# Eight tokens per one-hot operation, a 32-token top-k tile stacked on four partition sets, and early expert splits on GpSimd

## The chip, the cores and the metric

The kernel runs on one core of one Trainium2 chip. The core has five engines with queues of their own: TensorE (PE, with its weight load PEld), VectorE (DVE), ScalarE (ACT), GpSimd (POOL) and SyncE (SP, which here only issues DMAs). Each engine works through its queue in order and waits on semaphores for the others. The metric is the device time of one execution, in microseconds (us).

## What is computed

One layer of a decoder is run for 1024 prompt positions and 8 x 4 sample positions, 1056 tokens of 1024 features in all. A mixing part (RWKV-7 and a pooling part) comes first, then a PEER layer of 16384 single-neuron experts, then a gate and a last norm. The change lies in the PEER layer:

```python
q  = (xb @ wq).reshape(n, 8, 2, 128)             # 8 heads, two halves
s1 = einsum('thc,nc->thn', q[:, :, 0], sub_keys[0]); s2 = ... q[:, :, 1], sub_keys[1]
v1, i1 = top_k(s1, 16); v2, i2 = top_k(s2, 16)   # 16 of 128 keys, twice
cand = v1[..., :, None] + v2[..., None, :]       # 256 sums
sc, ci = top_k(cand.reshape(n, 8, 256), 16)      # 16 of them
expert = i1[ci // 16] * 128 + i2[ci % 16]
gate = softmax(sc)
act = gelu(einsum('thkd,td->thk', u_tab[expert], xb)) * gate
out = einsum('thk,thkd->td', act, v_tab[expert])
```

## The kernel before

The tokens stand in four groups (0-288, 288-544, 544-800, 800-1056; the sample comes first). For the first 672 tokens (`GA` to `GB`) the expert layer is done densely: a matrix G of 16384 experts x 672 tokens holds the gates, all experts are multiplied with all these tokens on PE, and G masks the result. For the other 384 tokens the chosen rows of the tables are gathered from memory by GpSimd and multiplied on DVE.

Ahead of the dense part three streams of work run interleaved (`merge`, lines 926 to 934, takes the next piece of the stream that is least far along by its stated length): `b_stream`, the RWKV chunks; `phase_c` of one group (output projection, norm, query projection, key scores, which go to memory in `sc_d`); and `t_stream` of the group before. `t_stream` runs `top` and `select` for each tile of up to 128 tokens that is dense: tiles of 128, 128 and 32 tokens in group 0, two of 128 in group 1, and one of 128 in group 2 (group 2 has 128 dense tokens). What was written in this order is then ordered anew by a scheduler when the program is built, engine by engine.

`top` (line 753) has the tokens on the partitions. For each of 16 rows of scores (8 heads x 2 halves) DVE takes eight largest, finds their places, strikes them out, takes the next eight and finds those: five operations (lines 762 to 767). `select` (line 772) builds 50 candidates a head (`cand` on DVE, their codes on GpSimd), finds 16 of them (lines 802 to 808, six operations a head), puts them in order of the code (lines 813 to 816, three a head), makes the softmax, and brings each gate to its place with a small one-hot `oh` (line 847 on DVE, then a product on GpSimd, then a sum at line 850).

For a dense tile the two key numbers and the gate of the 128 choices of each token are transposed on PE (line 863), so that the choices are on the partitions, and rounded to 16 bits (`e16`, the gate as a high and a low part). Then G is built four tokens at a time (lines 873 to 890): DVE compares a row 0..127 with both key numbers (line 882, 1024 elements a partition), multiplies the one-hot of the second key by the high part of the gate (line 883, 512 elements), and a third operation multiplies it by the low part (line 884, 512 elements). `GLO(t)` (line 1051) gives that one to DVE for every third set of four tokens and to GpSimd (the helper `PTT`, whose operations all have line 124) for the others. PE multiplies the one-hots, two matmuls a token (line 887), ACT moves the result out of PSUM into `gst` (line 889), and 32 tokens at a time it goes to `g_d` in memory (line 891). `ab`, the tile of the one-hots, has three buffers.

The dense part (`dense`, line 1170) takes 128 blocks of 128 experts. A block's `ublock` splits the weights into a high and a low part (`esplit`, line 1065: ACT makes `ehi`, and `elo` is made on DVE, line 1071, or on GpSimd), multiplies with all 672 tokens (`emm`, line 1093) and applies the GELU (line 1099). `ugate` multiplies by the rows of G (line 1150, loaded from `g_d` as `gq`) and splits again (`wh` on ACT, `wl` on DVE, line 1154). After eight blocks come eight `vblock`s. The first eight `ublock`s (`upre`) are run before G is complete, with GpSimd making `elo`; their results lie in `OT0` to `OT7`, of which `OT7` is in the pool `late`, in memory that the one-hot tiles give up. `gtop` runs `top` for the gathered tokens, three tiles of 128: the first before `dense(0, 18)` in the program, the two others after it.

## Time and profile before

| | us |
|---|---|
| median of 3 runs | 3357.13 |
| their range | 3352.67 to 3357.15 |
| the profiled execution | 3346.63 |
| its span, first to last instruction | 3344.9 |
| TensorE's granted clock, mean of the span | 0.98 |

The profile is of one execution. Its page gives the busy time of each engine and, in 40 equal slices of the span, the busy share in tenths. Times of day below are counted from the span's start. A matmul's record reaches to its end, and matmuls overlap, so a busy PE need not be one at its peak. A record of a DVE or GpSimd operation also holds the time in which it was started and could not go on.

In words: the mixing part and the first group's projections take the first 715 us; from there to 1394 us the streams run with `top`, `select` and the one-hots among them; from 1394 to 3230 us the dense part runs; a tail of norms and gates ends at 3345 us.

### The profile page before, as it was taken

The page shows a single profiled execution, that of the slowest core. Times are in us where ns is not written, and L with a number is a line of the kernel's source. Part 1 is how long each engine was busy: PE and PEld are TensorE (multiplying, and loading weights), DVE is VectorE, ACT ScalarE, POOL GpSimd, SP SyncE. Part 2 cuts the span into 40 slices and gives each one's busy share as a digit, 9 for nine tenths or more (in the row PEclk, how much of TensorE's full clock was granted, in tenths as well). Part 3 has the DMA queues.
Part 4 walks back from the last instruction along what each step waited for, and adds up shares of the span by engine and source line. Part 5 has one row for each costly group of instructions (what it writes and reads, how often), then busy time and mean ns, then how long its engine had stood idle before and what let it go on. Part 6 is the DMA issues. An engine that isn't in the chain of part 4 may idle for free.

```text
span 3344.9 us, 57622 instructions
## 1 busy us (share of the span) xinstructions
PE 3163.4 (95%) x21831; PEld 3063.6 (92%) x21831; DVE 2661.9 (80%) x5365; ACT 1187.9 (36%) x1778; POOL 1803.7 (54%) x1434
## 2 busy tenths in 40 slices
PE   8997999998888888999999999999999999999997
PEld 7886989988878777899999999999999999999997
DVE  6777332359999989889888888888889888888966
ACT  6452523345555555431222222122122222222243
POOL 5434333235565456337666666666566666666635
PEclk9998999999999989999999999999999999999998
DMA  5568645667677787639999999999999999999933
GB/s 176 204 218 199 170 134 144 196 193 228 199 198 232 207 290 222 233 128 366 341 339 328 344 349 331 329 340 334 336 337 350 325 335 339 342 328 341 324 110 128
DMA packets 467861, 883.61 MB, mean 264 GB/s; under 512 B 129280, under 2 KB 252416, under 8 KB 463104
## 3 DMA queue, kind: packets, MB, share of 16 engines
q1 hardware_dynamic: 356992, 477.24, 44.3%
q0 software_dynamic: 110592, 402.70, 32.8%
q8 instruction: 171, 2.80, 0.3%
q14 instruction: 106, 0.87, 0.1%
HBM read 759.22 MB, written 120.60 MB: 263 GB/s over the span
## 4 chain that ended last, share of the span: by engine, by line
PE 69%; DVE 16%; DMA 4%; POOL 2%; issue 2%; ACT 1%; SPq 0%; DVEq 0%; ACTq 0%; POOLq 0%
PE pd L1093 57%; DVE ab L882 3%; DVE ab L883 2%; PE ps L663 1%; PE ps L661 1%; PE ps L662 1%; PE ps L526 1%; DMA sraw<-wq 1%; PE ps L521 1%; DVE oh L847 1%; DVE h L718 1%; DVE I L763 1%; DVE s L765 1%; DVE ab L884 1%; DVE I L767 1%
## 5 line engine op out<-in xcount | busy, mean ns | idle before, releaser
L1202 POOL DMA_INDIRECT row<-v,idx x384 | 543.4, 1415 | 314.2 <-DVE po L1219 142.6
L1202 POOL DMA_INDIRECT row<-u,idx x384 | 536.4, 1397 | 284.9 <-DVE row L1210 112.3
L1069 ACT ACTIVATE ehi<-eraw 128x1024 fp32r<-128x1024 f32 x278 | 295.0, 1061 | 1098.3 <-PE pd L1093 955.2
L1093 PE MATMUL pd<-XH,elo 128*128 128x336 f32 x2176 | 516.2, 318 | 6.1 <-DVE elo L1071 3.2
L1093 PE MATMUL pd<-XL,ehi 128*128 128x336 f32 x2176 | 515.4, 318 | 0.0
L1093 PE MATMUL pd<-XH,ehi 128*128 128x336 f32 x2176 | 512.5, 316 | 0.0
L1093 PE MATMUL pd<-wh,ehi 128*128 128x336 f32 (+1 forms) x2112 | 503.0, 317 | 6.2 <-DVE tg L1283 6.2
L1093 PE MATMUL pd<-wl,ehi 128*128 128x336 f32 (+1 forms) x2112 | 503.1, 317 | 0.0
L1093 PE MATMUL pd<-wh,elo 128*128 128x336 f32 (+1 forms) x2112 | 503.0, 317 | 0.0
L1219 DVE SCALAR_TENSOR_TENSOR po<-row,act,po 128x1024 f32<-128x1024 f32 x381 | 488.5, 1282 | 6.5
L1210 DVE SCALAR_TENSOR_TENSOR row<-row,xt 128x1024 f32<-128x1024 f32 x384 | 455.2, 1220 | 5.9 <-DMA row<-u,idx 5.8
L1071 DVE TENSOR_TENSOR elo<-eraw,ehi 128x1024 fp32r<-128x1024 f32 x256 | 318.3, 1243 | 79.8 <-ACT ehi L1069 67.8
L1093 PEld LDWEIGHTS pd<-XH,elo 128*128 128x128 f32 x2176 | 373.8, 189 | 7.8 <-DVE elo L1071 4.3
L1093 PEld LDWEIGHTS pd<-XH,ehi 128*128 128x128 f32 x2176 | 373.0, 189 | 0.3
L1093 PEld LDWEIGHTS pd<-XL,ehi 128*128 128x128 f32 x2176 | 371.2, 189 | 0.2
L1093 PEld LDWEIGHTS pd<-wh,ehi 128*128 128x128 f32 x2112 | 361.5, 188 | 6.9 <-issue 6.7
L1093 PEld LDWEIGHTS pd<-wh,elo 128*128 128x128 f32 x2112 | 362.0, 188 | 0.2
L1093 PEld LDWEIGHTS pd<-wl,ehi 128*128 128x128 f32 x2112 | 361.8, 188 | 0.0
L124 POOL TENSOR_TENSOR ab<-ab,e 128x512 f16<-128x512 f16 x110 | 132.0, 1202 | 160.8 <-DVE ab L883 127.5
L1162 DVE TENSOR_TENSOR OT<-pd,OT 128x672 f32<-128x672 f32 x120 | 102.9, 857 | 139.6 <-PE pd L1093 138.0
L889 ACT ACTIVATE gst<-ps 128x512 f32<-128x512 f32 x168 | 177.1, 1093 | 74.0 <-PE ps L887 72.8
L661 PE MATMUL ps<-hi,whi 128*128 128x256 f32 (+1 forms) x592 | 180.0, 305 | 12.0 <-DMA whi<-wc_d 7.4
(504 smaller groups left out, 5849.7 us busy)
## 6 DMA issues: line engine op xcount, KB each, us to landing
eraw<-uT SPq DMA_DIRECT2D x128, 512.0 KB
eraw<-vP SPq DMA_DIRECT2D x128, 512.0 KB
g_d<-gst SPq DMA_DIRECT2D x21, 2048.0 KB
gq<-g_d SPq DMA_DIRECT2D x32, 1344.0 KB
whi<-wc_d SPq DMA_DIRECT2D x148, 256.0 KB
wlo<-wc_d SPq DMA_DIRECT2D x148, 256.0 KB
wc_d<-shi SPq DMA_DIRECT2D x40, 256.0 KB
wc_d<-slo SPq DMA_DIRECT2D x40, 256.0 KB
```

The lines of the kernel that those rows point to most:

```text
L124: nc.gpsimd.tensor_tensor(out, a, b, op=op)
L661: mm(ps[:, :n], whi[:, kk, :], xhi[:, k, :n], start=k == 0, stop=False)
L882: TT(ab[:, 0:4], iota16[:, None, :, :].to_broadcast([128, 4, EB, 2]), pairs(0, 4), op=ALU.is_equal)
L883: TT(ab[:, 4:6], ab[:, 2:4], pairs(2, 2), op=ALU.mult)
L889: ACT(st[:, :, t2:t2 + 4].rearrange("p e t -> p t e"), v3(ps, 128), AF.Copy, scale=1.0 / GS)
L1069: ACT(hi, raw, AF.Copy)
L1071: sub(lo, raw, hi.bitcast(F32), op=ALU.subtract)
L1093: mm(ps[:, a, :n], w_[:, k, :], x_[:, s:s + n], start=first, stop=last)
L1162: TT(halves(OT[db]), ps[:, :, :NH], halves(OT[db]), op=ALU.add)
L1202: nc.gpsimd.indirect_dma_start(out=r[:m], out_offset=None, in_=io[tab], in_offset=bass.IndirectOffsetOnAxis(ap=idx[:m, hh, k:k + 1], axis=0))
L1210: STT(r[:m], r[:m], 1.0, xt[:m], op0=ALU.mult, op1=ALU.mult, accum_out=pre[:m, k:k + 1])
L1219: STT(po[:m], r[:m], act[:m, k:k + 1], po[:m], op0=ALU.mult, op1=ALU.add)
```

## The change

Three things are changed, and one place in memory with them.

The one-hots are built for eight tokens an operation (`GT8`): the comparison has 2048 elements a partition, each product 1024. The third operation always goes to GpSimd, and `GLO` is gone. `ab` is twice as large and has two buffers in place of three. PE has as many matmuls as before and ACT as many moves, two PSUM banks for each set of eight.

The 32-token tile is stacked (`SH` = 4): the scores of two heads at a time lie on a set of 32 partitions, four sets on 128, so that `top` and `select` run over two heads in place of eight, on 128 partitions. Before the transposition the four sets are spread out into a zeroed tile `blk` (eight small ACT moves, one GpSimd memset), and three matmuls with `setsum`, a sum of four pieces of the identity, take the place of the three transpositions. Tiles of 128 tokens are done as before.

`dense(0, 18)` makes `elo` and `wl` on GpSimd (`PTT`) where DVE made them; the later blocks are as before. `OT6` joins `OT7` in `late`, since the larger `ab` leaves less memory. The length that `merge` is told for a tile falls from 24 + m/4 to 24 + m/8.

```diff
-    def top(tk, pos, m):
+    def top(tk, pos, mt):
+        src = sc_d[TIDX[pos]]
+        if mt > TC:
+            m, nh, loads = mt, HEADS, [(slice(0, mt), 0)]
+        else:
+            m, nh = mt * SH, HEADS // SH
+            loads = [(slice(g * mt, (g + 1) * mt), 2 * nh * g) for g in range(SH)]
-        for i in range(16):
+        for i in range(2 * nh):
...
-        for hh in range(HEADS):
+        for hh in range(nh):
...
+        if mt < m:
+            blk = tk.tile([128, HEADS, NCAND], F32, name="blk", tag="code").rearrange("p a b -> p (a b)")[:, :384]
+            nc.gpsimd.memset(blk, 0.0)
+            for g in range(SH):
+                r, c = slice(g * mt, (g + 1) * mt), slice(g * npr, (g + 1) * npr)
+                ACT(blk[r, 0:2, c], e12[r, :, :npr], AF.Copy)
+                ACT(v3(blk[r, 2, c], TOPK), gl[r, :nh, :], AF.Copy)
...
+                mm(ps[:, i * 128:i * 128 + mt], blk[:, i, :], setsum, start=True, stop=True)
...
-            for t2 in range(0, TC, 4):
+            for t2 in range(0, TC, GT8):
-                ab = gp.tile([128, 6, EB, 2], F16, name="ab", bufs=3)
+                ab = gp.tile([128, 3 * nb, EB, 2], F16, name="ab", bufs=2)
-                TT(ab[:, 0:4], iota16[:, None, :, :].to_broadcast([128, 4, EB, 2]), pairs(0, 4), op=ALU.is_equal)
-                TT(ab[:, 4:6], ab[:, 2:4], pairs(2, 2), op=ALU.mult)
-                GLO(t)(ab[:, 2:4], ab[:, 2:4], pairs(3, 2), op=ALU.mult)
+                TT(ab[:, 0:2 * nb], iota16[:, None, :, :].to_broadcast([128, 2 * nb, EB, 2]), pairs(0, 2), op=ALU.is_equal)
+                TT(ab[:, 2 * nb:], ab[:, nb:2 * nb], pairs(2, 1), op=ALU.mult)
+                PTT(ab[:, nb:2 * nb], ab[:, nb:2 * nb], pairs(3, 1), op=ALU.mult)
...
-    def GLO(t):
-        return PTT if t % 12 else TT
...
-            OT[db] = (dr if db < KB - 1 else late).tile([128, ND], F32, name=f"OT{db}")
+            OT[db] = (dr if db < KB - 2 else late).tile([128, ND], F32, name=f"OT{db}")
...
-        TT(wl, wt_, wh.bitcast(F32), op=ALU.subtract)
+        sub(wl, wt_, wh.bitcast(F32), op=ALU.subtract)
-    def vblock(g, db):
-        w = esplit(io["vP"][g, db])
+    def vblock(g, db, sub=TT):
+        w = esplit(io["vP"][g, db], sub)
...
-    dense(0, NB0)
+    dense(0, NB0, PTT)
```

The scheduler orders the program anew. The line numbers of the changed kernel are 2 to 25 higher for the same code. Up to the first tile of `t_stream` the engines have the same order but for the three small DVE operations that make `setsum`. Three places follow, of the kernel before first and then of the changed one.

GpSimd, about 1170 us in the profile before, where the one-hots of the last tile of group 1 run with little else (`ab` is the third one-hot product, `lo` and `sa` belong to `phase_c`, `elo` to the first expert blocks):

```order
L124 TENSOR_TENSOR X<-X,s__12346 128x256
L124 TENSOR_TENSOR yo<-yo,vgb 128x256
L124 TENSOR_TENSOR ab<-ab,e_12632 128x512 x12
L124 TENSOR_TENSOR lo<-y,hi 128x256 x3
L124 TENSOR_TENSOR ab<-ab,e_12632 128x512
L124 TENSOR_TENSOR lo<-y,hi 128x256
L124 TENSOR_TENSOR ab<-ab,e_12632 128x512
L124 TENSOR_TENSOR elo<-eraw,ehi 128x1024 x2
```
```order
L126 TENSOR_TENSOR X<-X,s__11905 128x256
L126 TENSOR_TENSOR ab<-ab,e_12323 128x1024
L126 TENSOR_TENSOR yo<-yo,vgb 128x256
L126 TENSOR_TENSOR ab<-ab,e_12323 128x1024 x9
L126 TENSOR_TENSOR lo<-y,hi 128x256 x2
L126 TENSOR_TENSOR ab<-ab,e_12323 128x1024
L126 TENSOR_TENSOR lo<-y,hi 128x256 x2
L126 TENSOR_TENSOR elo<-eraw,ehi 128x1024 x2
```

The products are twice as long. Eleven of them, for 88 tokens, stand where fourteen stood; those were for some 85 tokens, since every third set of four was DVE's.

ACT behind the last move of one-hots out of PSUM (`gst`), about 1362 us in the profile before (`q` and `scs` belong to `phase_c` of the last group, `ehi` to the weight splits, `OT` to the GELU of the first eight blocks):

```order
L889 ACTIVATE gst_13792<-ps_13891 128x4x128
L1069 ACTIVATE ehi_15047<-eraw_15045 128x1024
L742 ACTIVATE q_14806<-ps_14970 128x256
L750 ACTIVATE scs_15001<-ps_14996 128x512
L750 ACTIVATE scs_15009<-ps_15004 128x512
L1069 ACTIVATE ehi_15080<-eraw_15078 128x1024
L742 ACTIVATE q_15012<-ps_15019 128x256
L1069 ACTIVATE ehi_15136<-eraw_15134 128x1024
L742 ACTIVATE q_15012<-ps_15051 128x256
L1069 ACTIVATE ehi_15168<-eraw_15166 128x1024
L1099 ACT_TABLE_LOAD
L1099 ACTIVATE OT7_15132<-pd_15077 128x672
```
```order
L913 ACTIVATE gst_13321<-ps_13408 128x4x128
L1094 ACTIVATE ehi_14528<-eraw_14526 128x1024
L744 ACTIVATE q_14319<-ps_14394 128x256
L744 ACTIVATE q_14319<-ps_14362 128x256
L1094 ACTIVATE ehi_14560<-eraw_14558 128x1024
L744 ACTIVATE q_14319<-ps_14483 128x256
L1124 ACT_TABLE_LOAD
L1124 ACTIVATE OT6_14475<-pd_14420 128x672
L752 ACTIVATE scs_14514<-ps_14509 128x512
L752 ACTIVATE scs_14522<-ps_14517 128x512
L1094 ACTIVATE ehi_14593<-eraw_14591 128x1024
L744 ACTIVATE q_14525<-ps_14532 128x256
```

`OT6` now comes behind the last one-hots as well, and in all seven moves of `q` are left behind them where five were.

GpSimd in the early dense part, where the gathers of the first tile of gathered tokens begin (`oh` belongs to `gtop`, `row` is a gathered row of a table, `elo` and `wl` are the splits of the expert blocks):

```order
L124 TENSOR_TENSOR code<-code,iotaC 128x400
L124 TENSOR_TENSOR oh<-oh,gt 128x256 x8
L1202 DMA row<-u,idx_15448 128x1024 x16
L1202 DMA row<-v,idx_15448 128x1024 x16
L1202 DMA row<-u,idx_15448 128x1024 x16
```
```order
L126 TENSOR_TENSOR oh<-oh,gt 128x256
L1227 DMA row<-u,idx_14961 128x1024 x7
L126 TENSOR_TENSOR elo<-eraw,ehi 128x1024
L126 TENSOR_TENSOR wl<-wt,wh 128x672
L1227 DMA row<-u,idx_14961 128x1024 x2
L126 TENSOR_TENSOR elo<-eraw,ehi 128x1024
L1227 DMA row<-u,idx_14961 128x1024
L126 TENSOR_TENSOR wl<-wt,wh 128x672
L1227 DMA row<-u,idx_14961 128x1024 x4
L126 TENSOR_TENSOR elo<-eraw,ehi 128x1024
L126 TENSOR_TENSOR wl<-wt,wh 128x672
L1227 DMA row<-u,idx_14961 128x1024 x2
```

Where gathers followed gathers, fourteen `elo` and seven `wl` now stand among the first 53 of them; nine gathers and one `wl` later the gathers run alone as before.

## Rows read from the trace of the kernel before

**Rows 1.** The page: DVE's busy tenths in 40 slices of the span
```profile
DVE  6777332359999989889888888888889888888966
```

**Rows 2.** Busy us (x instructions) by stretch: PE, PEld, DVE, ACT, POOL; clock, DMA
```profile
715.00:1394.00 679.00, 582.93 (x5032) 543.39 (x5033) 628.19 (x2470) 368.24 (x587) 367.24 (x355) 0.96 0.75 227
1394.00:1510.00 116.00, 113.94 (x742) 113.41 (x740) 105.97 (x492) 42.33 (x58) 33.82 (x43) 1.00 0.38 136
1510.00:3230.00 1720.00, 1720.00 (x11205) 1719.95 (x11206) 1484.23 (x1769) 428.35 (x517) 1088.57 (x772) 1.00 0.91 331
```

**Rows 3.** The chain that ended last, 715 to 1394 us: shares by engine and line
```profile
by line: DVE ab L882 15.4%; DVE ab L883 9.0%; issue 4.4%; DVE oh L847 3.7%; DVE I L763 3.0%; DVE s L765 2.7%; DVE ab L884 2.7%; DVE I L767 2.7%; PE ps L887 2.5%; PE pd L1093 2.3%; DVE h L718 2.3%; DVE V L762 2.2%; DVE V L766 2.0%; DVE gl L8
```

**Rows 4.** What PE waited for, 715 to 1394 us: us in all, times, longest
```profile
PE ps L887 <- DVE ab L883: 28.5, 28, 3.0
PE ps L887 <- DVE ab L884: 10.8, 17, 1.3
PE ps L887 <- POOL ab L124: 9.9, 19, 2.4
```

**Rows 5.** Groups by line, 715 to 1394 us: busy us, mean ns, idle before
```profile
L882 DVE TENSOR_TENSOR ab<-iota,e 128x1024 f16<-128x1024 f16 x168 | 145.7, 878 | 15.7 <-PE ps L887 13.4 <-POOL ab L124 2.0
L883 DVE TENSOR_TENSOR ab<-ab,e 128x512 f16<-128x512 f16 x168 | 92.5, 561 | 0.3
L884 DVE TENSOR_TENSOR ab<-ab,e 128x512 f16<-128x512 f16 x58 | 35.0, 604 | 0.2
...
L124 POOL TENSOR_TENSOR ab<-ab,e 128x512 f16<-128x512 f16 x110 | 132.0, 1202 | 160.8 <-DVE ab L883 127.5 <-DVE K L816 10.1 <-DVE SC L806 6.5
```

**Rows 6.** By source line, whole span: ns shortest/median/longest, first and last start
```profile
L882 DVE TENSOR_TENSOR ab<-iota,e x168: 660/686/2337, 765.9 to 1353.7; 128x1024 f16<-128x1024 f16 x168
L883 DVE TENSOR_TENSOR ab<-ab,e x168: 390/416/2293, 772.8 to 1356.5; 128x512 f16<-128x512 f16 x168
...
L124 POOL TENSOR_TENSOR ab<-ab,e x110: 1030/1064/3525, 776.5 to 1357.1; 128x512 f16<-128x512 f16 x110
L124 POOL TENSOR_TENSOR elo<-eraw,ehi x22: 2349/2410/3056, 1200.5 to 3320.0; 128x1024 fp32r<-128x1024 f32 x22
```

**Rows 7.** Timeline, POOL and DVE at 1345 us: start us, us, instruction
```profile
1345.35 1.04 POOL L124 TENSOR_TENSOR ab<-ab,e 128x512 f16<-128x512 f16 x1 [1.02 <-DVE ab L883]
...
1345.46 1.48 DVE L882 TENSOR_TENSOR ab<-iota,e 128x1024 f16<-128x1024 f16 x1
```

**Rows 8.** The chain's pieces in order of time, 1340 to 1400 us: start, us
```profile
1347.60 0.33 DVE oh L847
1347.94 0.33 DVE ab L883
...
1350.69 0.87 DVE V L762 x4
...
1353.20 1.20 DVE ab L882 x2
...
1355.46 0.79 DVE I L763 x3
...
1363.69 8.04 DMA g_d<-gst
1372.16 10.03 DMA gq<-g_d
```

**Rows 9.** DVE's groups of the 32-token tile, 860 to 960 us: busy us, mean ns
```profile
L847 DVE TENSOR_TENSOR oh<-cF,CF 32x256 f32<-32x256 f32 x8 | 5.3, 677 | 0.2
L767 DVE FIND_INDEX8 I<-V,s 32x8 uint32<-32x128 f32 x16 | 4.3, 272 | 0.0
...
L850 DVE TENSOR_REDUCE gl<-oh 32x16 f32<-32x256 f32 x8 | 3.2, 399 | 0.0
...
L807 DVE FIND_INDEX8 CI<-SC,s 32x8 uint32<-32x50 f32 x8 | 1.5, 192 | 0.0
```

**Rows 10.** The page: one of the two groups of gathers: busy us, mean ns, idle before
```profile
L1202 POOL DMA_INDIRECT row<-v,idx x384 | 543.4, 1415 | 314.2 <-DVE po L1219 142.6
```

More of the change, by code (lines that the diff above doesn't have):

```diff
@@ L47 @@
 TC = 32
+GT8 = 8
+SH = 4
 NTC = ND // TC
@@ L768, in top, with select @@
             yield
-        yield from select(tk, pos, m, V12, I12)
-    def select(tk, col, m, V12, I12):
-        NSL = HEADS * TOPK
+        yield from select(tk, pos, mt, m, nh, V12, I12)
+    def select(tk, col, mt, m, nh, V12, I12):
+        sl = (slice(0, m), slice(0, nh))
         F12 = tk.tile([128, HEADS, 2, TOPK], F32, name="F12")
         for i in range(2):
-            ACT(F12[:m, :, i, :], I12[:m, :, i, :], AF.Copy, scale=1.0 if i else 128.0)
+            ACT(F12[:m, :nh, i, :], I12[:m, :nh, i, :], AF.Copy, scale=1.0 if i else 128.0)
         cand = tk.tile([128, HEADS, NCAND], F32, name="cand")
@@ L809, in select @@
             yield
-        STT(s3[:m], s3[:m], -BIG, code[:m], op0=ALU.is_equal, op1=ALU.mult)
+        STT(s3[sl], s3[sl], -BIG, code[sl], op0=ALU.is_equal, op1=ALU.mult)
         K16 = tk.tile([128, HEADS, TOPK], F32, name="K16")
-        for hh in range(HEADS):
+        for hh in range(nh):
             nc.vector.max(K16[:m, hh, 0:8], s3[:m, hh, :])
@@ L842, in select @@
         oh = {}
-        for h0 in range(HEADS + 1):
-            if h0 < HEADS:
+        for h0 in range(nh + 1):
+            if h0 < nh:
                 sh = [m, TOPK, TOPK]
@@ L1049, in body @@
     nc.vector.tensor_copy(iota16, it)
-    def GLO(t):
-        return PTT if t % 12 else TT
+    setsum = gp.tile([128, TC], F32, name="setsum")
+    TT(setsum, ident[:, 0:TC], ident[:, TC:2 * TC], op=ALU.add)
+    for g in range(2, SH):
+        TT(setsum, setsum, ident[:, g * TC:(g + 1) * TC], op=ALU.add)
     def xsplit():
@@ L1168, in vblock, with dense @@
             TT(OT[db], OT[db], ht, op=ALU.add)
-    def dense(b0, b1):
+    def dense(b0, b1, sub=TT):
         for b in range(b0, b1):
@@ L1173, in dense @@
                 if b not in U:
[L1174 to L1175 removed]
+                    ublock(b, sub)
+                ugate(b, sub)
             if b % VG == 0 and b:
                 for db in range(KB):
[L1178 removed]
+                    vblock(b // VG - 1, db, sub)
     NB0 = 2 * VG + 2
[L1181 removed]
+    dense(0, NB0, PTT)
     for col in range(128, GT, 128):
```

79 lines of the change are left out of this document (42 added, 37 removed).

## The prediction

> **What bounds the kernel now.** I read the page first, then the busy times by stretch, then the chain that ended last, the waits and the groups of the stretch that the change touches. From 1510 to 3230 us PE is busy in all of 1720 us, and from 1394 to 1510 us in 113.9 of 116 [rows 2]: in the dense part PE sets the time, and nothing that the change does there can give more than the 2 us that are open. The stretch to look at is 715 to 1394 us, where DVE is busy for 628 of 679 us and PE for 583 [rows 2]; on the page DVE's slices stand at 8 and 9 there [rows 1]. The chain of this stretch runs mostly over DVE, with the one-hots (L882, L883, L884) at 27.1% of it, 184 us [rows 3], and PE's longest waits are for one-hots: 28.5 and 10.8 us for DVE, 9.9 us for GpSimd [rows 4]. So DVE is the bound here, at 92.5% busy, and PE is the next, with 96 us idle; that is the most the stretch can give while PE's work stays as it is.
>
> One more thing must be read before DVE's time is added up. The comparison takes 686 ns in the median but 878 in the mean, the product of 512 elements 416 and 561 [rows 5, 6]. Two neighbours show why: a comparison that starts 0.1 us after a GpSimd product of 1.04 us takes 1.48 us [rows 7]. It did not run beside the product; it ran after it. By mean less median the 168 comparisons hold 32 us of such waiting, the 168 products 24 us, and the 58 third operations on DVE, taking the same 416 for them, 11 us: 67 us.
>
> **What is taken from DVE.** *Longer operations.* On the chain one comparison takes 0.60 us from start to start and one product 0.33 [rows 8]; the records are some 0.08 us longer, since the next operation starts before they end. Half the elements cost 0.27 us less, so 0.06 us of each is fixed. A set of eight takes 0.06 + 2 x 0.54 = 1.14 us for the comparison and 0.60 for the product, where two sets of four take 1.20 and 0.66. That is 0.12 us for each of 84 sets, 10 us. By the lengths of the records (686 and 416, fixed part 0.146) it would be 0.29 us a set, 24 us; I take 10, since it is starts that fill an engine.
>
> *The third operation.* 58 of them leave DVE, at 0.33 us: 19 us (their waiting is counted below).
>
> *The 32-token tile.* Its operations cost what those of a full tile cost, since time goes by the elements of a partition: 272 ns for a search in 128 scores of 32 tokens [rows 9]. On the chain four MAX8 take 0.87 us and three searches 0.79 [rows 8], so one of the sixteen rounds of `top` takes 2 x 0.22 + 3 x 0.26 = 1.22 us (the strike-out counted as a search). Twelve rounds go: 15 us. A head of `select` has nine operations on 50 candidates, 0.11 us each (192 ns by its record [rows 9], less the overlap) and 0.06 us more for those that load values, say 1.2 us, and the small one-hot and its sum, 0.33 us each: 1.9 us, and six heads go: 11 us. Together 26 us; by lengths of records and means (0.677 and 0.399 us for the last two [rows 9]) it would be 37. Against it stand a memset on GpSimd and eight small ACT moves, once, on engines at 367 and 368 of 679 us [rows 2]: nothing, unless PE waits for them, which would be 2 or 3 us.
>
> So DVE's own work falls by 10 + 19 + 26 = 55 us (up to 80 by the records).
>
> **What is put on GpSimd.** 110 products at 1.06 us become 84 of 1024 elements, which the trace does not show. The nearest rows are the 512-element product at 1.06 us, which bounds it at 2.13, and `elo`, 1024 elements of four bytes, at 2.41 [rows 6]; if the fixed part were half of the 512-element time, it would be 1.6. I take 2.1, nearest to the row with the same type: 176 us in place of 117. GpSimd has room (367 of 679 us [rows 2]), but what it holds DVE cannot use. The waiting of DVE's one-hots, 67 us now, is bounded from both sides: if it goes with DVE's own time on them (146 us after, 175 before) it falls to 56; if it goes with GpSimd's time on its product, it rises by half, to 100. The middle is 78, 11 us more. DVE's busy time in the stretch so falls by 55 - 11 = 44 us, with 55 - 33 = 22 and 55 + 11 = 66 as bounds. At the same busy share of 92.5% the stretch is shorter by 48 us.
>
> [...]
>
> **What is given back.** On PE the second matmul of each token needs GpSimd's product, which ends about 1.1 us later than before. PE waited for it 19 times, 9.9 us [rows 4]; I count 4 us more. Behind the last one-hots, the order of ACT shows seven moves of `q` where five were: two more blocks of `phase_c`, 48 matmuls, at 1720 us for 11205 of the larger ones [rows 2] at most 7 us before the dense part; I take 6. The write of G and the first load from it, 8.0 and 10.0 us [rows 8], stay under that work and two expert blocks as before. `OT6` now waits for memory that the one-hots release; its matmuls' result lies in one of two PSUM buffers, and PE has the other block and `phase_c` to do meanwhile, so I cost it at nothing; without that cover it is the 8 us of the write.
>
> *The early splits.* 26 `elo` and 18 `wl` go to GpSimd, 2.41 us and, by elements of the same row, 1.6 us each. An expert block keeps PE for 48 matmuls of 0.153 us, 7.4 us. What DVE is spared gives PE at best the 2 us open at 1394 to 1510 us. What GpSimd is given costs nothing while it stands alone, but the order puts the last fourteen `elo` and seven `wl` among 53 gathers: 53 x 1.42 [rows 10] + 14 x 2.41 + 7 x 1.6 = 120 us in one queue, while fourteen blocks last 103 on PE. The 17 us over are met by the lead, some 4 us (a block's time less the two splits of its weights) and what the first seven gathers with free buffers can run ahead. With each gather's waiting (314 us for 384, 0.8 us each [rows 10]) the queue would be 45 us longer. The bounds are 0 and 50; I take 12, near the lower end, because DVE, which those gathers wait for, has less to do here.
>
> **Sum.** 48 - 4 - 6 - 12 = 26 us. The profiled execution takes 3346.6 us (span 3344.9), so 3320.6; it is 10.5 us under the median of the runs, 3357.1. Against the median the forecast is **3331 us**, 0.8% faster.
>
> **The rivals.** *More of it.* The waiting does not grow (DVE gains 66 us) and nothing is given back: 66/0.925 = 71 us, 3286 us. For it: GpSimd starts half as often on a thing that DVE wants. Against it: each hold is twice as long. Chance 0.15.
>
> *The shared path sets the pace: slower.* Counted as one queue, the two-input operations of both engines take for eight tokens 1.20 + 0.66 + 0.69 x 0.33 + 1.31 x 1.06 = 3.48 us before (58 and 110 operations in 84 sets) and 1.14 + 0.60 + 2.1 = 3.84 after, 30 us more in all; the tile gives back some 6. This case ends 24 us later: 3381 us. It decides once the waiting of the one-hots rises from 67 us to over about 120, that is, once it eats the 55 us. For it: DVE's idle time is small and its order puts the comparison of the next set beside the product of this one. Against it: much of DVE's time in the stretch is MAX8 and searches of one input. [...] Chance 0.08.
>
> *GpSimd's queue holds the expert blocks.* The splits among the gathers come 45 us late in all: 48 - 10 - 45 = 7 us slower, 3364 us. For it: fourteen blocks' worth of the queue is over-full by the rows. Against it: the lead, and gathers are shortest (0.9 us) when their row is free. Chance 0.10.
>
> *The gain is hidden.* PE's waits for DVE's one-hots (39 us [rows 4]) turn into waits for GpSimd's, in a queue that cannot pass over them, and of the tile's 26 us some 20 are given back as above: about 5 us, 3352 us. For it: PE is at 86% by its records. Against it: waits for one-hots are what PE waits for most. Chance 0.12.
>
> **How the numbers follow.** The forecast has 0.55. Its own range comes from the bounds of DVE's relief, 22 to 66 us (24 to 71 in the stretch), less the 22 given back: 3308 to 3355. For 8 in 10 the range takes in the first rival and reaches to the third: 3287 to 3364; the shared path and the far ends are left out. Within 0.2% (7 us, about what a measurement of this kernel can tell from no change) lies the hidden case; the third rival is just beyond it, and I split its chance: faster 0.70, same 0.14, slower 0.16.
>
> **What would show it.** In the changed profile the one-hots should be 84 comparisons with a median near 1.2 us, 84 products near 0.69, and GpSimd's 84 near 2.1; the difference of mean and median on DVE should hold about 80 us. The first `vblock` should start near 1355 us in place of 1395, and in the next 200 us PE should lose some 10 us to waits for GpSimd's `elo`. DVE's operations on 32 partitions should be gone. The forecast is wrong if GpSimd's product is far over 2.4 us, if the waiting exceeds 120 us, if PE's waits for GpSimd's product grow to tens of us, or if the waits for `elo` are nothing or several times what I take.

## The result, and the profile after

The changed kernel takes 3403.1 us (median of 4 runs, 3398.5 to 3407.6) where the kernel before takes 3357.1. The ratio is 1.014, with a 95% interval of 1.0124 to 1.0155: 46 us slower, where 26 us faster was forecast. The profiled execution of the changed kernel has a span of 3404.5 us; it lies 3 us above the median of its runs, while the profiled execution of the kernel before lies 10.5 us below the median of its own, so the two profiles differ by 60 us.

The page's busy tenths of DVE and POOL in 40 slices, kernel after (a slice is 85 us):

```profile
DVE  6777333259988799686988888888888888888856
POOL 5434233236575466569766665666566666666435
```

Beside [rows 1], DVE has 6 to 8 in places where it had 8 and 9. POOL has a 9 where the expert part begins (the slice from 1532 to 1617 us), which it had nowhere before. The same in busy time by stretch, kernel after; columns as in [rows 2]. The first row answers to 715 to 1394 there, the second to the first 190 us of the expert part, and the last line is the kernel before in those 190 us:

```profile
715.00:1408.00 693.00, 596.04 (x5088) 563.41 (x5087) 594.35 (x2055) 367.21 (x603) 414.86 (x329) 0.93 0.75 225
1408.00:1640.00 232.00, 198.87 (x1194) 192.73 (x1193) 180.26 (x550) 52.30 (x70) 180.84 (x128) 0.93 0.59 196
1640.00:3290.00 1650.00, 1650.00 (x10744) 1649.96 (x10743) 1406.54 (x1669) 414.05 (x500) 1029.44 (x727) 1.00 0.90 326
```

```profile
1394.00:1585.00 191.00, 188.94 (x1220) 188.41 (x1219) 173.58 (x576) 56.79 (x75) 89.45 (x81) 0.99 0.61 226
```

The two profiles differ in two places. The stretch of the one-hots ends 14 us later, at 1408 us, although DVE is busy for 34 us less in it [rows 2]: its end did not come earlier. Some 5 of these 14 us stand ahead of the first search of a score tile (it starts at 642.3 us, before at 637.1), where the two programs have the same order but for three small operations; the run e2_no_splits below shows by medians that this first place is worth about 2 us and not 14. And behind it PE needs 232 us for 1194 matmuls, where it did 1220 in 191: 41 us more, with POOL busy for 181 us instead of 89. From 1640 to 3290 us PE is busy without a gap.

The operations of the change themselves came out near what was forecast. By source line, kernel after: ns shortest/median/longest, first and last start (the comparison, the product, and the product on POOL):

```profile
L904 DVE TENSOR_TENSOR ab<-iota,e x84: 1162/1324/3217, 771.2 to 1359.4; 128x2048 f16<-128x2048 f16 x84
L905 DVE TENSOR_TENSOR ab<-ab,e x84: 635/691/2654, 780.0 to 1362.1; 128x1024 f16<-128x1024 f16 x84
L126 POOL TENSOR_TENSOR ab<-ab,e x84: 1882/1893/3660, 782.6 to 1363.0; 128x1024 f16<-128x1024 f16 x84
```

Against [rows 6]: 1.32 us where 1.2 was said, 0.69 where 0.69 was said, 1.89 where 2.1 was said. What DVE and PE waited for, 715 to 1408 us, kernel after (us in all, times, longest):

```profile
DVE V L771 <- DMA scq<-sc_d: 22.8, 5, 14.8
DVE ab L904 <- PE ps L912: 18.9, 14, 4.1
DVE S L615 <- PE ps L613: 18.5, 2, 9.9
```

```profile
PE ps L912 <- ACT gst L913: 28.3, 32, 4.3
PE ps L912 <- POOL ab L126: 14.1, 16, 1.9
PE ps L912 <- DVE ab L905: 13.6, 6, 6.7
```

DVE now waits for work that PE has to do first: the scores of the next tile (22.8 us, 2.0 before; they are a load that stands behind PE's projections), a free buffer of one-hots (18.9, 13.4 before), the state of the recurrence (18.5, which is not among its ten largest waits before). PE's waits for DVE fell from 28.5 and 10.8 us [rows 4] to 13.6, but a wait for ACT's move out of PSUM has taken their place, 28.3 us in 32 times where it was 8.0 in 12. PE's waits for one-hots and their moves are 57 us in sum before and 56 after.

The second place, PE from 1408 to 1640 us, and the timelines of POOL, ACT (one row) and PE around its longest wait there (start us, us, instruction, idle time before it):

```profile
PE pd L1118 <- POOL elo L126: 20.8, 8, 9.0
PE pd L1118 <- ACT OT L1189: 7.2, 1, 7.2
```

```profile
1503.25 1.06 ACT L1094 ACTIVATE ehi<-eraw 128x1024 fp32r<-128x1024 f32 x1 [0.89 <-PE pd L1118]
...
1510.51 1.92 POOL L1227 DMA_INDIRECT row<-u,idx  x1 [0.30 <-issue]
1512.45 2.35 POOL L126 TENSOR_TENSOR elo<-eraw,ehi 128x1024 fp32r<-128x1024 f32 x1
1514.75 1.61 POOL L126 TENSOR_TENSOR wl<-wt,wh 128x672 fp32r<-128x672 f32 x1
1516.52 1.75 POOL L1227 DMA_INDIRECT row<-u,idx  x1 [0.16 <-issue]
```

```profile
1505.39 0.46 PE L1118 MATMUL pd<-XL,ehi 128*128 128x336 f32 x2
1514.85 0.93 PE L1118 MATMUL pd<-XH,elo 128*128 128x336 f32 x2 [9.00 <-POOL elo L126]
1515.58 0.76 PE L1118 MATMUL pd<-XH,ehi 128*128 128x336 f32 x2
1516.14 0.76 PE L1118 MATMUL pd<-XL,ehi 128*128 128x336 f32 x2
...
1518.44 0.47 PE L1118 MATMUL pd<-XH,ehi 128*128 128x336 f32 x2
1518.75 0.47 PE L1118 MATMUL pd<-XL,ehi 128*128 128x336 f32 x2
```

Here POOL does one thing after the other without waiting for anybody, and PE stands for 9.00 us until the split that it needs has its turn behind the gathers. ACT has no other `ehi` between 1503.25 us and the start of this `elo` at 1512.45, so what the `elo` needs of ACT was ready by 1504.3, and PE was through with all that came before by 1505.9; from then on, for more than 6 us, only gathers kept it. When PE goes on, two matmuls take 0.56 us from start to start, and 0.31 a few us later: the granted clock is 0.66 in 1505 to 1520 us. From 1514.85 to 1518.44 us seven such pairs take 3.6 us, where they would take 2.2 at 0.31, so the slow matmuls cost 1.4 us on top of this wait. So in this trace POOL took the `elo` in the order of its queue: it stood more than 6 us behind gathers while all that it needs was ready.

### The profile page after: what moved, and what is told of

It reads as the page before. It is cut to its first block, busy times and chain, and to the rows that moved or that the text cites. A ratio compares the mean times of both kernels' runs of the same rounds, so it can differ in the third digit from the quotient of the medians.

```text
span 3404.5 us, 57141 instructions
## 1 busy us (share of the span) xinstructions
PE 3185.1 (94%) x21834; PEld 3087.5 (91%) x21834; DVE 2627.7 (77%) x4906; ACT 1178.5 (35%) x1784; POOL 1942.1 (57%) x1447
## 4 chain that ended last, share of the span: by engine, by line
PE 55%; DVE 2%; POOL 1%; issue 1%; DMA 0%; ACT 0%; ACTq 0%; DVEq 0%; POOLq 0%
PE pd L1118 54%; POOL elo L126 1%; POOL row L1227 1%; DVE OT L1324 0%; DVE cand L802 0%; DVE tg L1310 0%; DMA row<-u,idx 0%; DVE oh L856 0%; DVE wt L1175 0%; DVE wl L1276 0%; PE ps L665 0%; PE ps L663 0%; DVE GH L1324 0%; PE ps L664 0%; POOL wl L126 0%
## 5 line engine op out<-in xcount | busy, mean ns | idle before, releaser
L1227 POOL DMA_INDIRECT row<-u,idx x384 | 545.4, 1420 | 279.3 <-DVE row L1235 102.8
L1244 DVE SCALAR_TENSOR_TENSOR po<-row,act,po 128x1024 f32<-128x1024 f32 x381 | 499.8, 1312 | 10.9 <-DMA row<-v,idx 4.5
L1235 DVE SCALAR_TENSOR_TENSOR row<-row,xt 128x1024 f32<-128x1024 f32 x384 | 465.4, 1246 | 16.5 <-DMA row<-u,idx 15.5
L1096 DVE TENSOR_TENSOR elo<-eraw,ehi 128x1024 fp32r<-128x1024 f32 x230 | 284.7, 1238 | 73.9 <-ACT ehi L1094 68.0
L126 POOL TENSOR_TENSOR ab<-ab,e 128x1024 f16<-128x1024 f16 x84 | 169.5, 2021 | 140.9 <-DVE ab L905 127.4
```

The costliest lines, as they stand in the source:

```text
L126: nc.gpsimd.tensor_tensor(out, a, b, op=op)
L1096: sub(lo, raw, hi.bitcast(F32), op=ALU.subtract)
L1227: nc.gpsimd.indirect_dma_start(out=r[:m], out_offset=None, in_=io[tab], in_offset=bass.IndirectOffsetOnAxis(ap=idx[:m, hh, k:k + 1], axis=0))
L1235: STT(r[:m], r[:m], 1.0, xt[:m], op0=ALU.mult, op1=ALU.mult, accum_out=pre[:m, k:k + 1])
L1244: STT(po[:m], r[:m], act[:m, k:k + 1], po[:m], op0=ALU.mult, op1=ALU.add)
```

## The experiments

All ratios are to the kernel before on the same chip, whose median was 3360 to 3361 us there.

| run | us | ratio, 95% interval |
|---|---|---|
| e1_splits | 3404.7 | 1.0128, 1.0111 to 1.0146 |
| e2_no_splits | 3363.7 | 1.0007, 0.9997 to 1.0017 |
| e8_wl_only | 3368.2 | 1.0022, 1.0013 to 1.0031 |
| e3_tile | 3372.8 | 1.0032, 1.0021 to 1.0042 |
| e4_eight | 3373.3 | 1.0033, 1.0022 to 1.0044 |
| e5_less_dve | 3378.0 | 1.0050, 1.0036 to 1.0064 |
| e6_less_pe | 3372.9 | 1.0031, 1.0021 to 1.0041 |
| e7_two_products | 3352.1 | 0.9969, 0.9957 to 0.9981 |
| e9_order | 3369.8 | 1.0024, 1.0015 to 1.0033 |
| e10_tile_order | 3365.3 | 1.0015, 1.0007 to 1.0024 |
| e11_less_dve_order | 3371.2 | 1.0035, 1.0022 to 1.0047 |
| e12_two_products_order | 3347.0 | 0.9953, 0.9941 to 0.9966 |
| e13_before_len20 / 26 / 32 | 3381.5 / 3387.2 / 3371.9 | 1.0071 / 1.0089 / 1.0025, each within 0.0023 |
| e14_no_splits_len20 / 26 / 32 | 3365.6 / 3369.7 / 3368.3 | 1.0017 / 1.0031 / 1.0022, each within 0.0016 |

### The early splits

e1_splits is the kernel before with

```
-    dense(0, NB0)
+    dense(0, NB0, PTT)
```

and the parameter `sub` handed on, as in the change. e2_no_splits is the changed kernel with this line put back.

> The kernel before with one part of the change alone: the 26 weight remainders and 18 product remainders of the first expert blocks go to GpSimd. Theory A (the splits stand in one queue with the gathers and hold the expert blocks): the stretch after the first expert block lengthens by 40 to 50 us, and the time is 3357 + 45 = about 3400 us, with GpSimd over 80% busy while the splits last. Theory B (the splits are covered, and the loss comes from the one-hots' late end): 3350 to 3360 us.

> The changed kernel with the early splits back on DVE, the eight-token one-hots and the stacked tile kept. Theory A (the splits cost about 45 us by themselves): 3403 - 45 = 3358 us or up to 10 us less, so no better than the kernel before, since its first expert block starts 13 us later than before in the trace. Theory B (the splits are covered): 3390 to 3403 us, as the changed kernel.

Theory A held in both: 1.28% slower with the splits alone, and with all the rest no better than the kernel before and not measurably slower (3363.7 us, 6 above the 3358 of the theory). 1.0140 over 1.0007 is 1.0133, so the splits cost 44 us in the one kernel and 45 in the other; the parts add up. Another order ahead of the splits is no rival here: by the traces PE, DVE, ACT and POOL do the same work in the same order up to the last one-hot in e1_splits as in the kernel before, and in e2_no_splits as in the changed kernel. Busy time by stretch, from the last comparison to the 24th expert block: first e1_splits, then the kernel before; and PE's waits in e1_splits from 1365 to 1640 us:

```profile
1365.00:1552.00 187.00, 159.57 (x1024) 154.39 (x1023) 138.58 (x588) 58.61 (x82) 122.71 (x88) 0.95 0.52 177
```

```profile
1354.00:1507.00 153.00, 148.70 (x1014) 147.10 (x1015) 127.59 (x589) 59.53 (x81) 45.57 (x49) 1.00 0.48 174
```

```profile
PE pd L1093 <- POOL elo L124: 25.9, 14, 6.5
PE pd L1093 <- ACT OT L1164: 7.4, 1, 7.4
```

34 us lie here: PE idle for 27 us instead of 4, and 11 us longer busy for about the same matmuls, at a clock of 0.95 instead of 1.00. To the start of the 35th block, behind the last block with an early split, it is 48 us (279 instead of 231). These are single executions, and that of the kernel before is a fast one, so the profiles differ by more than the 44 us of the medians.

e8_wl_only is the changed kernel with

```
-    dense(0, NB0, PTT)
+    dense(0, NPRE, PTT)
+    dense(NPRE, NB0)
```

so that of its 44 early splits only eight `wl`, ahead of the first gather, are on GpSimd. The 14 `elo` and 8 `wl` that stood among the gathers are back on DVE, but so are 12 `elo` and two `wl` that stood ahead of them.

> The changed kernel with only the first eight product remainders on GpSimd, which stand ahead of the first gather in its queue; all later early splits are back on DVE. Theory Q (what costs is standing among the gathers, not being on GpSimd): as the kernel with all early splits on DVE, 3364 us, within 6 us. Rival (each split is dearer on GpSimd and holds the expert blocks wherever it stands): 8 of the 44 splits, 8 us or more slower, over 3371 us.

3368 us, 4.5 above e2_no_splits: within the 6 us of theory Q, though the two intervals hardly overlap and the 5 us may be real. That all of the 44 us comes from splits among the gathers doesn't follow, since 14 others were put back as well. The traces of the changed kernel and of e2_no_splits show how much does. In both the first row goes from the first `vblock` to ten blocks later, shortly ahead of the first gather (1501 us in the changed kernel), the second over the next fifteen blocks; first the changed kernel, then e2_no_splits:

```profile
1408.50:1495.60 87.10, 78.15 (x482) 76.19 (x481) 79.52 (x444) 25.13 (x37) 51.61 (x48) 0.94 0.24 70
1495.60:1641.80 146.20, 122.02 (x723) 117.85 (x721) 102.47 (x109) 26.74 (x33) 130.02 (x83) 0.92 0.81 273
```

```profile
1407.50:1481.30 73.80, 73.80 (x481) 73.80 (x481) 71.54 (x410) 24.52 (x34) 12.37 (x24) 1.00 0.27 83
1481.30:1598.10 116.80, 112.64 (x723) 112.02 (x721) 100.07 (x165) 29.09 (x37) 77.04 (x57) 0.99 0.85 310
```

For the same matmuls, 29 us are lost among the gathers and 13 ahead of them. The 13 have another cause, which the changed kernel's timeline shows (the last row is of DVE in e2_no_splits):

```profile
1406.34 12.77 POOL L126 TENSOR_TENSOR wl<-OT,wh 128x672 fp32r<-128x672 f32 x8 [3.33 <-ACT wh L1177]
1419.08 2.35 POOL L126 TENSOR_TENSOR elo<-eraw,ehi 128x1024 fp32r<-128x1024 f32 x1
1413.46 8.03 DVE L802 TENSOR_TENSOR cand<-V 128x64 f32<-128x64 f32 x5
1422.48 0.76 ACT L1177 ACTIVATE wh<-wt 128x672 fp32r<-128x672 f32 x1 [10.08 <-DVE wt L1175]
1427.24 0.93 PE L1118 MATMUL pd<-wh,ehi 128*128 128x336 f32 x2 [7.19 <-ACT OT L1189]
...
1405.28 5.47 DVE L1179 TENSOR_TENSOR wl<-OT,wh 128x672 fp32r<-128x672 f32 x7 [1.89 <-ACT wh L1177]
```

Eight `wl` take 12.8 us on GpSimd, and seven of them 5.5 on DVE. While they and the `elo` behind them last, five `cand` of DVE take 8.03 us, 1.65 each in the median where all 63 of this kernel have a median of 0.27, and end with the `elo`; they did not run beside GpSimd's work, as the comparison in [rows 7] did not. So DVE's product `wt` comes late, ACT's `wh` waits 10.1 us for it, ACT's move of the first `vblock` out of PSUM stands behind that `wh`, and PE waits 7.2 us for the move. In e8_wl_only, with the same eight `wl`, the same ten blocks take 82.1 us, 8 more than in e2_no_splits, and the next fifteen 111.1, 6 less: theory Q held in the total, but what the `wl` cost at their place was for the most part made up later.

### The tile and the one-hots, one at a time

e3_tile is the kernel before with the changes in `top` and `select` and with `setsum`; the loop over four tokens, three buffers and `GLO` stay. e4_eight is the kernel before with the loop over `GT8` tokens alone.

> The kernel before with one part of the change alone: the 32-token top-k tile stacked on four partition sets. Theory T (the 26 us that DVE is spared shorten the stretch, and something else in the change eats them): 3357 - 26 = about 3331 us, at least 10 us faster than before. Rival (DVE's relief at this place turns into waits of its own for the tile's loads and small moves): 3350 to 3360 us.

> The kernel before with one part of the change alone: one-hots for eight tokens an operation in two buffers, their third operation all on GpSimd. Theory W (the longer sets make new waits, for the two buffers, for GpSimd's long product and for the two PSUM moves, that cost more than DVE is spared): 15 to 30 us slower, 3372 to 3387 us, with DVE's waits for PE and PE's waits for ACT grown. Rival (DVE's relief of 29 us less the waiting counts, as predicted): 3335 to 3350 us.

Both are 11 us slower than the kernel before, though each takes work from DVE. For the tile theory T fell, and so did its rival, by which nothing would have been gained or lost. For the one-hots 3373 us lies in the range of theory W, but 11 us is less than the 15 to 30 that it gave; PE's waits for ACT grew as it said (29.6 us from 8.0), DVE's for PE did not (6.7 us for a buffer, 13.4 before). Part of the loss shows in DVE's groups of operations that neither kernel's change touches, 715 to 1400 us (busy us, mean ns), first before, then e4_eight:

```profile
L847 DVE TENSOR_TENSOR oh<-cF,CF 128x256 f32<-128x256 f32 (+1 forms) x56 | 34.4, 627 | 2.2 <-ACT cF L824 1.3
L793 DVE TENSOR_TENSOR cand<-V 128x64 f32<-128x64 f32 (+11 forms) x49 | 17.3, 397 | 0.0
```

```profile
L848 DVE TENSOR_TENSOR oh<-cF,CF 128x256 f32<-128x256 f32 (+1 forms) x56 | 57.6, 1042 | 1.9 <-ACT cF L825 1.0
L794 DVE TENSOR_TENSOR cand<-V 128x64 f32<-128x64 f32 (+11 forms) x49 | 32.5, 699 | 0.0
```

The same 56 and 49 two-input operations take 38 us more. Counted in the trace, every one of them that is longer than 0.7 us overlaps an operation of GpSimd; 17 stand behind GpSimd's product, which now lasts 1.9 us, and take 31 us, where it was 8 operations and 8 us before. The rest of the 38 us, some 15, stands behind GpSimd's other work, whose place in the order has changed. That e2_no_splits, with both edits, is 9 us better than either alone says that the sum of parts does not hold here. As I read it, something else moves with each edit.

### Less work for one engine, nothing else

In e5_less_dve all strike-outs of the score tiles go, 144 of them, of which 124 start ahead of 1394 us in the profile before (the first edit; the second eight values then repeat the first, so it leaves out a part of the layer). In e6_less_pe every second product with the activations' low part goes (the second):

```
-            nc.vector.match_replace(s2[:m], v8[:, 0:8], s_, -BIG)
-            nc.vector.max(v8[:, 8:16], s2[:m])
-            nc.vector.max_index(i8[:, 8:16], v8[:, 8:16], s2[:m])
+            nc.vector.max(v8[:, 8:16], s_)
+            nc.vector.max_index(i8[:, 8:16], v8[:, 8:16], s_)
...
+            if k % 2 == 0 or n == XW:
+                mm(ps[:, :n], whi[:, kk, :], xlo[:, k, :n], start=False, stop=False)
```

> The kernel before with 120 strike-outs of the score tiles left out (the second eight values and indices are searched in the same scores again, so they repeat the first eight), and nothing else: about 31 us less for DVE in the stretch by starts (120 x 0.26), no other engine's work changed. Theory D, the prediction's (DVE bounds the stretch, and its relief shortens it at the same busy share): 31 / 0.925 = 34 us faster, about 3325 us. Theory H (DVE and PE hand work to each other in two fixed orders, so what one saves it waits for the other): at most 10 us faster, 3350 to 3360 us, with DVE's idle time in the stretch up by 20 us or more.

> The kernel before with half of the products of the weights with the low part of the activations left out in the projections ahead of the top-k (every second one of 128 rows), and nothing else: 240 matmuls of 256 columns at 0.12 us from start to start, 29 us less for PE in the stretch, and some 7 us less before it. Theory D (DVE bounds the stretch): only what lies before the stretch and behind the last one-hots counts, 8 to 15 us faster, 3345 to 3352 us. Theory P (PE's order bounds it, also where DVE is 90% busy): 29 + 7 = 36 us faster, 3324 us. Theory H (both, in turns): between, and in either case PE's relief is worth more than the same relief of DVE.

Every forecast of the time missed: with some 30 us less for DVE the kernel is 17 us slower, with 29 us less for PE 10 us slower. Only the sign that theory H named for e5_less_dve came, DVE's idle time up by more than 20 us (26 in the stretch below). Busy time by stretch, 715 to 1400 us, in e5_less_dve, e6_less_pe and the kernel before:

```profile
715.00:1400.00 685.00, 589.05 (x4870) 551.97 (x4870) 607.52 (x2196) 359.00 (x575) 358.57 (x352) 0.89 0.72 217
```

```profile
715.00:1400.00 685.00, 566.33 (x4657) 519.41 (x4656) 631.16 (x2415) 359.93 (x576) 359.01 (x354) 0.90 0.73 218
```

```profile
715.00:1400.00 685.00, 588.93 (x5071) 549.39 (x5072) 633.68 (x2478) 374.24 (x596) 367.24 (x355) 0.96 0.75 227
```

In e5 PE has as many busy us as before and 201 matmuls fewer to show for them; the granted clock is 0.89 where it was 0.96. So a loss on PE stands against DVE's gain. And PE's queue holds other work at other places: of the projections' 2496 matmuls, counted in the traces in PE's order, 2391 stand ahead of the last one-hot in the kernel before, 2328 in e2, 2304 in e4, 2292 in e3 and in e5. As I read it, what is left behind it is done when DVE has nothing more to give. Each of these edits changes the times by which the program's order is planned, and so the order of all engines.

### The order alone

Four runs make the same edit of the order, in four kernels named above (before, e3, e5, e7):

```
-            for _ in streams[0][1]:
-                pass
+            up = upre()
+            merge([streams[0], (CL[step], islice(streams[1][1], 24)), (8, islice(up, 6))])
```

> The kernel before with its work unchanged and another order: in the last step the projections and the first six expert blocks are merged with the last one-hots instead of standing behind them in the program, so that in PE's order 2496 of the projections' 2496 matmuls stand ahead of the last one-hot instead of 2391 (and 338 of the expert blocks' instead of 336). Theory O (order: work that PE finds between its waits is free, work left behind the last one-hots is paid): up to 105 x 0.12 = 13 us faster, 3347 us. Rival (what is set ahead holds the one-hots back by as much): 3355 us or more.

> The stacked tile alone (3373 us), with the same change of order: 2496 of the projections' matmuls ahead of the last one-hot instead of 2292, and 381 of the expert blocks' instead of 336. Theory O (DVE is spared 26 us by the tile, but the order that comes with it leaves 99 more projections' matmuls behind the last one-hots than the kernel before, so nothing comes of it): the 204 x 0.12 + 45 x 0.15 = 31 us come back in part, at least 12 of them: 3342 to 3361 us. Rival (order is not what eats it): 3368 us or more.

> The kernel before with 120 strike-outs left out (3378 us), with the same change of order: 2496 of the projections' matmuls ahead of the last one-hot instead of 2292. Theory O: 204 x 0.12 = 24 us come back in part, at least 12 of them, 3354 to 3366 us, and the relief of 31 us of DVE shows once it is not bought with work left for the end: below the kernel before in its new order by 5 us or more. Rival (DVE's relief buys nothing in any order): not faster than the kernel before in its new order.

e9_order is 0.24% slower, against theory O: its last comparison starts 24 us later after the first search than before, so what was set ahead held the one-hots back. e10 and e11 are 6 and 5 us faster by the ratios than the same kernels without it, half of what theory O said; e10 lies between theory O and its rival. e11 is not below e9, as its rival said: that relief of DVE bought nothing in either order. So a count of matmuls behind the last one-hot does not by itself tell the time. What these runs do show is that order is worth 5 to 8 us with the work unchanged.

The last six runs draw the order anew with the smallest edit that does it, the constant in `t_len` (20, 26, 32 for 24), in the kernel before and in e2_no_splits; no instruction is added or removed.

> The kernel before, the same instructions, with the constant 24 in the length of the top-k stream set to 20: a new order of all queues, 2297 of the projections' matmuls ahead of the last one-hot instead of 2391. Theory N (the order of the kernel before is an unusually good one, and any edit loses it): 94 x 0.12 = 11 us slower, 3368 to 3378 us. Rival (order is worth nothing, the time is set by the work): 3360 us within 5.

> The kernel before, the same instructions, with the constant 24 set to 26: 2280 of the projections' matmuls ahead of the last one-hot instead of 2391. Theory N: 111 x 0.12 = 13 us slower, 3368 to 3380 us. Rival: 3360 us within 5.

> The kernel before, the same instructions, with the constant 24 set to 32: 2371 of the projections' matmuls ahead of the last one-hot instead of 2391, the nearest to the kernel before of the three. Theory N: least slower of the three, 3360 to 3370 us. Rival: 3360 us within 5, as the other two.

> The kernel with eight-token one-hots and the stacked tile, early splits on DVE (3364 us), with the same constant set to 20: 2304 of the projections' matmuls ahead of the last one-hot. Theory N: 3358 to 3370 us, and over the three constants 5 to 15 us below the kernel before with the same constants, which is then what the edits are worth. Rival (the edits are worth nothing in any order): at or above the kernel before with the same constants.

> The kernel with eight-token one-hots and the stacked tile, early splits on DVE, with the constant set to 26: 2316 of the projections' matmuls ahead of the last one-hot. Theory N: 3358 to 3370 us, below the kernel before with the same constant. Rival: at or above it.

> The kernel with eight-token one-hots and the stacked tile, early splits on DVE, with the constant set to 32: 2304 of the projections' matmuls ahead of the last one-hot. Theory N: 3358 to 3370 us. Rival: at or above the kernel before with the same constant.

Theory N held in its direction: the same work in three other orders takes 24, 30 and 8 us longer than the kernel before by the ratios, and all three times lie above N's ranges, by 2 to 7 us. A count of matmuls behind the last one-hot does not give the time here either: 20 more are left there in e13_before_len32, at 0.12 us each, and it is 8 us slower. The three runs of e2's work lie in N's ranges, but at 32 its interval and that of the kernel before overlap. With e9 there are four other orders of before, at 1.0024 to 1.0089 (mean 1.0052), and four of e2's work, at 1.0007 to 1.0031 (mean 1.0019). Like for like the one-hots and the tile are then worth 0.33%, 11 us; by the three pairs with the same constant 18, 20 and 1 us. But the kernel before has a fifth order, its own, at 1.0000, as e2's own is counted among its four; with it the mean is 1.0042 and the edits are worth 8 us. With so few orders, scattered over 30 us, a gain of some 10 us is the best estimate, but even its sign is not shown. Busy time from 78 us after the start of the first search to the last comparison, in the kernel before, e13_before_len26 and e14_no_splits_len26:

```profile
715.00:1354.00 639.00, 547.22 (x4753) 509.04 (x4753) 603.57 (x2369) 351.04 (x563) 352.80 (x348) 0.95 0.75 223
```

```profile
721.00:1368.00 647.00, 545.62 (x4665) 506.49 (x4664) 621.00 (x2381) 347.68 (x559) 342.67 (x349) 0.93 0.73 214
```

```profile
722.00:1368.00 646.00, 540.12 (x4697) 508.93 (x4695) 589.90 (x1962) 343.65 (x567) 396.98 (x318) 0.94 0.73 217
```

In the new order before's DVE is busy for 17 us more with the same work, and PE does 88 matmuls fewer by then. With the edits DVE has 31 us less to do than that, and the length is the same.

### The long hold, and a faster kernel

e7_two_products is e2_no_splits with GpSimd's product cut in two:

```
-                PTT(ab[:, nb:2 * nb], ab[:, nb:2 * nb], pairs(3, 1), op=ALU.mult)
+                e3 = e16[:, t // GT8, 3:4].rearrange("p j (a b) -> p (j a) b", b=2)
+                for hb in (0, nb // 2):
+                    PTT(ab[:, nb + hb:nb + hb + nb // 2], ab[:, nb + hb:nb + hb + nb // 2],
+                        e3[:, hb:hb + nb // 2, None, :].to_broadcast([128, nb // 2, EB, 2]), op=ALU.mult)
```

> The changed kernel with the early splits on DVE, and GpSimd's product of 1024 elements cut into two of 512 elements. Theory L (the long hold of the shared path is what costs: DVE's other two-input operations wait up to 1.9 us for it): holds of 1.0 us instead of 1.9 bring 5 to 15 us, about 3350 us. Rival (the hold's length is paid once either way, two operations add a fixed part each): 3360 to 3370 us, as the kernel with the same splits and the product in one piece, 3364 us.

> The kernel with eight-token one-hots, the stacked tile, early splits on DVE and GpSimd's product in two pieces (3352 us), with the same change of order: 2452 of the projections' matmuls ahead of the last one-hot instead of 2349, 288 of the expert blocks' instead of 336. Theory O: 103 x 0.12 - 48 x 0.15 = 5 us, 3347 us or a little less. Rival (what is set ahead holds the one-hots back): 3352 us or more.

Theory L held for e7: 0.31% faster than the kernel before and 12 us below e2, below all four orders of e2's work, though its own order is a new one too. POOL's product by source line, and PE's waits for one-hots and moves, 720 to 1400 us, e7:

```profile
L126 POOL TENSOR_TENSOR ab<-ab,e x168: 1029/1040/2146, 783.6 to 1357.9; 128x512 f16<-128x512 f16 x168
```

```profile
PE ps L915 <- POOL ab L126: 32.8, 42, 2.0
PE ps L915 <- DVE ab L905: 11.0, 10, 2.5
PE ps L915 <- ACT gst L916: 8.6, 11, 3.0
```

The two halves take 2.08 us instead of 1.89, and still it is faster. But the cause that L named is not shown: DVE's `oh` and `cand` take 43.5 and 23.4 us, in e2 36.4 and 29.3, so their waits did not fall in sum. What fell is PE's wait for ACT's move, from 28.6 us in e2 to 8.6: as I read it, PE gets the first half of a set earlier, so the matmuls of its two halves come less close together. The wait for POOL's product rose from 14.4 to 32.8. With DVE's (14.7 and 11.0) that is 52 us against 58, so these waits alone don't give the 12 us; how much of the 12 us is a luckier order stays open. With the edit of the order on top, e12 is 0.47% faster than the kernel before, and 1.8% below the changed kernel. The 5 us by which it is below e7 are what theory O gave there.

## Why the prediction was wrong, step by step

The forecast and the result are 72 us apart. By the runs 32 of them are the splits, 44 us where 12 were said, and 40 the rest, 2 us slower (e2_no_splits) where 38 faster were said.

**DVE's relief came out within its bounds.** DVE is busy for 34 us less in the stretch; 44 was said, with 22 to 66 as bounds. The three durations were right to about 10%. The waiting of the one-hots, mean less median, is 25 us for the comparisons (84 times 1.618 less 1.324) and 25 for the products (84 times 0.993 less 0.691): 50, not 78. But DVE's other two-input operations wait too (105 of them take 38 us more in e4_eight, and five `cand` 8.03 us above), so the waiting was counted in too few places. The second rival, the shared path as the pace, did not come: no 120 us.

**"At the same busy share" is the step that failed first.** 44 us of relief were turned into 48 us of time by holding DVE at 92.5%. Measured, its share fell to 594.35 of 693 us, 86%, and the first `vblock` starts at 1408 us, not at 1355. DVE and PE work for each other in two fixed orders, and the time that DVE saves comes back as waits for the tile's scores, for buffers and for the recurrence (22.8, 18.9 and 18.5 us), all behind PE. That relief of DVE need not shorten the stretch is shown twice without the change (e5 and e11). In the order in which it was built the rest of the change brings nothing, and over several orders some 10 us by the best estimate, not 38 (48 less the 10 given back). The fourth rival, with 5 us, was nearer, at a chance of 0.12, but not by its mechanism: PE's waits for DVE turned for the most part into waits for ACT's moves, not for GpSimd.

**What was given back** was right for PE's wait for POOL (14.1 us, where 9.9 and 4 were said) and for the projections left behind the last one-hots (63 matmuls more, 8 us, where 6 were said). That PE waits for ACT's moves out of PSUM, 28.3 us where it was 8.0, was not among the steps; that the two moves of a set now follow at once is the likely reason.

**The order of the kernel before was taken as given.** The sum starts from its time and changes the work. But an edit also gives up its order, and the four others of the same work that were run are 8 to 30 us slower. I read the changed order for places and never asked what the old one was worth. Nothing in one trace tells this; one more order of the same work would have.

**The early splits: 12 was taken from 0 to 50, and 44 is what they cost.** The arithmetic of the queue was there: 120 us of POOL's work against 103 on PE. Measured, the same 53 gathers, 14 `elo` and 7 `wl` are busy for 120 us and take 134, some 0.2 us between any two, so the queue is 31 us over. Nothing of it was met by a lead: PE loses 29 us over these blocks. That the lead would meet the 17 us for the most part is the step that failed here, and the reason for the low end, that DVE has less to do, was beside the point: POOL hardly waited for anybody. The other 13 us were lost ahead of the first gather, where the prediction put the splits at nothing ("costs nothing while it stands alone"): there GpSimd's long `wl` (12.8 us for eight) hold DVE (8.03 us for five `cand`), and through DVE and ACT also PE (7.2 us). The third rival had the place of most of it and the size, 45 us, at a chance of 0.10, but the size by luck: its own rows, 17 us over and 0.8 us of waiting for each of 53 gathers, give about 60, the gathers had 0.2 between them, and the 13 us ahead of them it did not have.

**The rivals were taken as excluding each other.** The third and the fourth have different places, and something near both came: 3352 plus 45 is 3397, six under what was measured. No sum of the prediction takes two of them together, and its range ends at 3364.

## What to carry to other kernels

In this kernel an instruction put on the engine that issues gathers cost its place in that queue, not its duration (the 44 early splits 44 us together, the eight ahead of the gathers, by themselves, 4.5): add up the queue over the stretch against the consumer's work, and take the excess as lost until a lead is shown. Ahead of the gathers, look also at what a long GpSimd operation holds on DVE (here 8.03 us for five `cand`), and who waits for that. Relief of an engine that was 92% busy brought nothing here, in two orders (e5_less_dve 17 us slower than before, e11 not below e9); look at what the relieved engine will wait for next. Where an edit makes a planner order all queues anew, time two or three neutral orders of the old kernel before a difference of under 1% is put down to the work.

## What the runs showed that was not expected

Taking work from PE did not free it: e6_less_pe has 414 matmuls fewer than before in 715 to 1400 us, 8% of them, and is busy for 22.6 us less, 4%, at a granted clock of 0.90 instead of 0.96. In 1180 to 1210 us, where PE is busy for 15.0 of 30 us, its granted clock there is 0.50. In e5_less_dve an edit of DVE's work alone, and the new order with it, brought PE's clock in the stretch from 0.96 to 0.89. So a matmul's price in such a stretch was not fixed (0.116 us of PE's busy time before, 0.122 in e6, 0.121 in e5), and in this kernel the clock belongs to the account of an edit that moves the waits between matmuls.
